# Attention probabilities turned by VectorE and DRAM transfers instead of TensorE, in a two-layer hybrid model on one Trainium2 core

## The chip, the core and the metric

The kernel runs on one core of one Trainium2 chip. The metric is the device time of one execution in microseconds (us), taken as the median of several runs. The profile is one execution taken by the hardware profiler; its span, from the first instruction to the last, is a little shorter than the device time of the same execution.

The engines are named as the profile names them: PE is TensorE (PEld its weight loads), DVE is VectorE, ACT is ScalarE, POOL is GpSimd, SP is SyncE. SP issues the weight loads as DMAs. DMAs issued from POOL go through a queue of their own ("q0 software_dynamic" in the profile), those of SP through "q1 hardware_dynamic"; all run on the core's 16 DMA engines.

## The reference

A model of two layers over 512 tokens of width 1024, all in float32. Layer one is attention over three groups of heads ("dilated" windows), layer two an mLSTM; each is followed by a SwiGLU network, and a norm ends it. Only the attention is touched here. Cut to what matters:

```python
proj = (xn @ w_in).reshape(B, S, 3, 3, 8, 128)           # group, q/k/v, head
for g, (window, dilation) in enumerate(((128, 1), (512, 4), (2048, 16))):
    q = rope(proj[:, :, g, 0]) * scale; k = rope(proj[:, :, g, 1]); v = proj[:, :, g, 2]
    s = where(valid, q @ k.T, -inf)      # banded, in blocks of 128
    p = exp(s - max(s)); den = sum(p)
    outs.append((p / den) @ v); lses.append(max(s) + log(den))
wts = softmax(stack(lses), axis=0)       # over the three groups
o = einsum('gbsh,gbshd->bshd', wts, stack(outs))
h = h + o.reshape(B, S, 1024) @ w_out
```

## The kernel before, in words

**Stages.** Activations are kept transposed (features on the 128 partitions, 512 tokens in the free dimension). Every projection is a product in three parts of rounded operands: a weight chunk of 512 KB (four row blocks of 128, 256 columns) is loaded by SP (line 200), split into a high part by ACT (line 208) and a low part by DVE (line 209), and multiplied by PE as high by high, high by low and low by high (lines 239 and 271). Three buffers of each kind (`W_BUFS`) let the load and the split run ahead of PE. A "tick" is one such chunk; `advance()` counts them, and `defer(n, fn)` runs `fn` once n more ticks have passed.

**Attention.** `attention_pair(pr)` (line 529) treats two heads at a time, four times. It projects q and k of the three groups (12 chunks), then v of the three groups (6 chunks). The work on the scores is deferred and falls among these chunks: `scores0` and `scores12` (products, masks, row maxima, exponentials), then `weigh` (exchange of maxima and sums between layouts, then one factor per row and block on DVE, lines 638 and 641), `turn` (values of group 0 turned by PE), `transposes(i)` for each of the pair's two heads and `values(i)`. The ticks are in `RUN_AT` (line 36), and in `LAST_AT` for the last pair. `run` and `fenced` hold PE's work of such a piece together at its place in the order.

**The turn of the probabilities.** A head has 15 blocks of 128 by 128 probabilities: 7 of group 0 (`p0`) and 4 each of groups 1 and 2 (`p12`). The values product contracts over keys, so each block is needed with the keys on the partitions. `transposes(i)` (line 652) turns 15 blocks on PE into four PSUM banks, and ACT copies each bank to SBUF (line 660) into one of four `pt` buffers. `values(i)` (line 663) multiplies: 7 products for group 0 (line 672), 8 for groups 1 and 2 (line 677), into the one PSUM bank of tag `t`; ACT copies the result to `oT` (line 679). As there are four `pt` buffers, the second head's blocks are turned after the first head's values product, in the same piece.

**The end of the attention.** For the last pair the pieces stand at the last v chunks and in the first chunk of the output projection. Lines 741 to 747 split six heads' outputs into high and low parts (lines 223, 224) before that projection, and the last two in a deferred piece. `out_project` (line 754) makes one column group of 256 after the other: two chunks, two accumulators.

**The start.** Line 108 keeps PE busy with 9 idle products while the first data come.

**Order.** Each engine works strictly in its own order; the build places instructions on each engine by their priority and an estimate of when they are ready. Tiles with one tag share `bufs` buffers in turn.

Of the kernel before, what the change touches and what calls it, by code (L numbers as in the profile page):

```python
# [11 lines left out]
F32 = mybir.dt.float32  # L12
# [58 lines left out]
def tile_hybrid_dilated_attn_mlstm(  # L71
# [33 lines left out]
    def idle(n):  # L105
        for i in range(n):
            nc.tensor.matmul(idle_ps, ones_r, idle_w, start=True, stop=True)
# [126 lines left out]
    def multiply(acc, whl, pairs, ch, m, nk):  # L234

        for k in range(min(4, nk - 4 * ch)):
            kk = 4 * ch + k
            for a, b in SPLITS:
                nc.tensor.matmul(  # L239
                    acc, whl[a][:, k, m * P:(m + 1) * P], pairs[b][kk],  # L240
                    start=(kk == 0 and (a, b) == SPLITS[0]),
                    stop=(kk == nk - 1 and (a, b) == SPLITS[-1]))
# [78 lines left out]

    with ExitStack() as actx:
        ap = pool(actx, "attn")

        R = 32
        mask_part = cst[:, K_MB:K_MB + 4]
        acst = ap.tile([P, K_END - K_MA], F32, name="acst")
        part = lambda at, w: acst[:, at - K_MA:at - K_MA + w]
        mask_band, mask_causal, mask_dil, perm = part(K_MA, 2 * P), part(K_M1, P), part(K_M2, P), part(K_G, P)
        cosn = ap.tile([R, SEQ], F32, name="cosn")  # L330
        sinn = ap.tile([R, SEQ], F32, name="sinn")
        sinr = ap.tile([R, SEQ], F32, name="sinr")

        posi = ap.tile([P, SEQ], I32, tag="rt", name="posi", bufs=2)
# [31 lines left out]
                nc.gpsimd.tensor_copy(cosn[:, c * P:(c + 1) * P], cs[s])  # L366

        def tok_tile(name):
            return ap.tile([P, 2, SEQ], F32, tag="qk", name=name, bufs=8)


        xtok = ap.tile([P, TB, D], F32, tag="heads", name="x_tok")
# [58 lines left out]

        def squares(hf):
            for tb in range(TB):
                sq = ap.tile([P, 512], F32, tag="v", name="x_sq", bufs=4)
# [94 lines left out]
        def attention_pair(pr):  # L529
# [6 lines left out]
            p0, p12, pts, vt = {}, {}, {}, []  # L536

            def score_bank(i, name):
                return ps.tile([P, 512], F32, tag="so"[i], name=name, bufs=2)
# [1 line left out]
            def scores0(q, k):  # L541

                for i in range(2):
                    p0[i] = ap.tile([P, 7, P], F32, tag="p0", name="%sp0_%d" % (nm, i), bufs=2)
                    for b2 in range(2):
                        sp = score_bank(i, "%ss0" % nm)
                        o, parts = 0, []
                        for b in (2 * b2, 2 * b2 + 1):
                            lo_ = max(b - 1, 0) * P
                            w = (b + 1) * P - lo_  # L550
                            nc.tensor.matmul(sp[:, o:o + w], q[:, i, b * P:(b + 1) * P],
                                             k[:, i, lo_:lo_ + w], start=True, stop=True)
                            parts.append((b, o, w))
                            o += w
                        for b, o, w in parts:
                            pb = max(2 * b - 1, 0)
                            nc.vector.tensor_tensor_reduce(
                                p0[i][:, pb:pb + w // P, :].rearrange("p a b -> p (a b)"),
                                sp[:, o:o + w], mask_band[:, 2 * P - w:], 1.0, -3e38,
                                op0=ALU.add, op1=ALU.max, accum_out=own[:, 0, 0, i, b:b + 1])  # L560
                for i in range(2):
                    exponentials(0, i)

            def scores12(qk1, qk2):

                for i in range(2):
                    p12[i] = ap.tile([P, 8, P], F32, tag="p12", name="%sp12_%d" % (nm, i), bufs=2)
# [49 lines left out]
            def weigh():  # L617

                exchange()
                cf = ap.tile([P, 16], F32, tag="cf", name=nm + "cf", bufs=2)  # L620
# [12 lines left out]
                cf4 = cf.rearrange("p (o i b) -> p o i b", o=2, i=2)  # L633
                for i in range(2):
                    for b in range(4):
                        pb = max(2 * b - 1, 0)
                        blk = p0[i][:, pb:2 * b + 1, :].rearrange("p a b -> p (a b)")
                        nc.vector.tensor_scalar(blk, blk, cf4[:, 0, i, b:b + 1], None, op0=ALU.mult)
                    for c in range(4):
                        blk = p12[i].rearrange("p (g c) k -> p c g k", g=2)[:, c]  # L640
                        nc.vector.tensor_scalar(blk, blk, cf4[:, 1, i, c:c + 1], None, op0=ALU.mult)

            def turn():
                for i in range(2):
# [17 lines left out]

            def values(i):
                pt = pts[i]
                hs = slice(i * P, (i + 1) * P)
                op = ps.tile([P, 512], F32, tag="t", name=nm + "o", bufs=1)
                first = True
                for b in range(4):
                    for kb in range(max(b - 1, 0), b + 1):
                        idx = 2 * b - (b - kb)  # L670
                        src = pt[idx // 4][:, (idx % 4) * P:(idx % 4 + 1) * P]
                        nc.tensor.matmul(by_block(op)[:, b], vt[0][:, kb, hs], src,
                                         start=first, stop=False, skip_group_check=True)
                        first = False
                for g in (1, 2):
                    for c in range(4):
                        nc.tensor.matmul(op[:, c * P:(c + 1) * P], vt[g][:, c, hs], pt[1 + g][:, c * P:(c + 1) * P],
                                         start=False, stop=(g == 2 and c == 3), skip_group_check=True)
                nc.scalar.activation(o_head(2 * pr + i), op, AF.Copy)

            qks = []
            for g in range(3):
# [30 lines left out]
                if g == 0:  # L713
                    defer(RUN_AT[0], lambda: run(lambda: scores0(*qks[0])))
            later_runs = (
                (lambda: scores12(*qks[1:]),), (weigh, turn),
                (lambda: transposes(0),), (lambda: values(0), lambda: transposes(1)), (lambda: values(1),))
            for at, fns in zip(RUN_AT[1:] if pr < HEADS // 2 - 1 else LAST_AT, later_runs):
                defer(at, lambda fns=fns: run(*fns))
            for g in range(3):  # L720
                v = ap.tile([P, TB, 256], F32, tag="v", name="%sv%d" % (nm, g), bufs=4)
                vt.append(v)

                def evac_v(m, acc, v=v):
# [10 lines left out]
                    project(pair, w_in, 2 * D + pr * 256, KC, evac_f, nm + "g0v")  # L735
                else:
                    project_tokens(pair, w_in, g * 3 * D + 2 * D + pr * 256, evac_v, "%sg%dv" % (nm, g))

        for pr in range(HEADS // 2):
            attention_pair(pr)  # L740
# [4 lines left out]
        def last_heads():  # L745
            for k in range(HEADS - 2, HEADS):
                split_act(pair[0][k], pair[1][k], o_head(k), None)

        def add_to_h(c):
            def evac(m, acc):  # L750
# [469 lines left out]
```

## Time and profile before

| | us |
|---|---|
| median of 3 runs | 1479.23 (1479.03 to 1479.31) |
| device time of the profiled execution | 1479.76 |
| its span | 1478.0 |
| PE busy | 1467.8 |
| DVE busy | 769.0 |
| ACT busy | 544.9 |
| POOL busy | 103.4 |

A row of the profile's groups reads: line, engine, operation, output<-inputs, shapes, count | busy time of the group, mean duration of one | idle time of the engine before them. PE's products are pipelined: each is listed with its full duration and they overlap, so what one costs PE is the distance from its start to the next start. A group's busy time is the union of its instructions. A row of the timeline has start, length, engine, line, operation; neighbours of one kind are merged with their count, and a bracket at the end tells the idle time before and what ended it. A row of the DMA view has the size of one transfer in KB and the median time from its issue to its landing. Of the span, the attention with its output projection takes the first 525 us.

### The profile page before, as it was taken

How to read it: one execution, taken by the hardware profiler on the slowest of the kernel's cores; microseconds unless marked ns; L12 is line 12 of the kernel's file. 1: busy time of each engine (PE TensorE's matmuls, PEld its weight loads, DVE VectorE, ACT ScalarE, POOL GpSimd, SP SyncE). 2: the span in 40 equal slices, each digit the busy share in tenths (PEclk: the TensorE clock that was granted, in tenths of full speed). 3: DMA queues.
4: the chain of work that ended last, by engine and by line, in shares of the span. 5: the costliest groups of instructions: out<-in, count | busy, mean ns of one | idle time of the engine just before them, and what ended most of it. 6: DMA issues, size and time to landing. Idle time of an engine off the chain costs nothing. (4 is left out here: it accounts for less than half of the span.)

```text
span 1478.0 us, 18932 instructions
## 1 busy us (share of the span) xinstructions
PE 1467.8 (99%) x7497; PEld 1253.0 (85%) x7497; DVE 769.0 (52%) x1515; ACT 544.9 (37%) x997; POOL 103.4 (7%) x95
## 2 busy tenths in 40 slices
PE   9999999999999999999999999999999999999998
PEld 7899889889889888888888889798888888888887
DVE  8744654654665463444343338987755443343233
ACT  5343225225216342333222223785542333233223
POOL 1000000000000001111110000000000111110001
PEclk9999999999999999999999999999999999999999
DMA  6222222232232233333323232232233233332231
GB/s 199 86 86 72 86 86 73 85 100 72 72 100 72 73 97 102 90 96 100 100 91 95 93 98 83 62 97 58 81 105 100 90 96 100 100 93 93 86 100 72
DMA packets 128466, 134.45 MB, mean 91 GB/s; under 512 B 5429, under 2 KB 121461, under 8 KB 128377
## 3 DMA queue, kind: packets, MB, share of 16 engines
q1 hardware_dynamic: 126384, 131.55, 28.7%
q8 instruction: 59, 0.97, 0.3%
q10 hardware_dynamic: 1656, 1.12, 0.2%
q0 software_dynamic: 336, 0.57, 0.1%
q14 instruction: 31, 0.25, 0.1%
HBM read 131.12 MB, written 2.10 MB: 90 GB/s over the span
## 5 line engine op out<-in xcount | busy, mean ns | idle before, releaser
L239 PE MATMUL f0j<-n_h,f0j_h 128*128 128x512 f32 x352 | 137.1, 389 | 0.0
L239 PE MATMUL f1j<-n_h,f1j_h 128*128 128x512 f32 x352 | 137.1, 389 | 0.0
L239 PE MATMUL f0j<-n_h,f0j_l 128*128 128x512 f32 x352 | 137.0, 389 | 0.0
L239 PE MATMUL f1j<-n_h,f1j_l 128*128 128x512 f32 x352 | 137.0, 389 | 0.0
L239 PE MATMUL f0j<-n_l,f0j_h 128*128 128x512 f32 x352 | 136.9, 389 | 0.0
L239 PE MATMUL f1j<-n_l,f1j_h 128*128 128x512 f32 x352 | 136.9, 389 | 0.0
L209 DVE TENSOR_TENSOR f1j_l<-f1j_w,f1j_h 128x1024 fp32r<-128x1024 f32 x44 | 54.9, 1247 | 54.5 <-ACT f1j_h L208 54.5
L209 DVE TENSOR_TENSOR f0j_l<-f0j_w,f0j_h 128x1024 fp32r<-128x1024 f32 x44 | 54.8, 1245 | 54.5 <-ACT f0j_h L208 54.5
L239 PEld LDWEIGHTS f0j<-n_h,f0j_l 128*128 128x128 f32 x352 | 66.1, 188 | 13.9
L239 PEld LDWEIGHTS f1j<-n_h,f1j_l 128*128 128x128 f32 x352 | 66.1, 188 | 13.8
L239 PEld LDWEIGHTS f1j<-n_h,f1j_h 128*128 128x128 f32 x352 | 66.1, 188 | 13.8
L239 PEld LDWEIGHTS f0j<-n_h,f0j_h 128*128 128x128 f32 x352 | 66.1, 188 | 13.8
L239 PEld LDWEIGHTS f1j<-n_l,f1j_h 128*128 128x128 f32 x352 | 66.1, 188 | 13.5
L239 PEld LDWEIGHTS f0j<-n_l,f0j_h 128*128 128x128 f32 x352 | 66.1, 188 | 13.5
L208 ACT ACTIVATE f1j_h<-f1j_w 128x1024 fp32r<-128x1024 f32 x44 | 46.5, 1057 | 73.3 <-PE f1j L239 72.2
L208 ACT ACTIVATE f0j_h<-f0j_w 128x1024 fp32r<-128x1024 f32 x44 | 46.5, 1057 | 73.3 <-PE f0j L239 72.2
L1152 PE MATMUL fin<-fw_h,f1ah 128*128 128x512 f32 (+1 forms) x198 | 72.8, 368 | 0.0
L1152 PE MATMUL fin<-fw_l,f1ah 128*128 128x512 f32 (+1 forms) x198 | 72.5, 366 | 0.0
L1152 PE MATMUL fin<-fw_h,f1al 128*128 128x512 f32 (+1 forms) x198 | 72.4, 366 | 0.0
L239 PE MATMUL fo<-f0ah,fo_k_h 128*128 128x512 f32 x176 | 68.5, 389 | 0.0
L239 PE MATMUL fo<-f0al,fo_k_h 128*128 128x512 f32 x176 | 68.5, 389 | 0.0
L239 PE MATMUL fo<-f0ah,fo_k_l 128*128 128x512 f32 x176 | 68.5, 389 | 0.0
(1167 smaller groups left out, 3579.8 us busy)
## 6 DMA issues: line engine op xcount, KB each, us to landing
f0j_w<-in_ffn_w_in_dram SPq DMA_DIRECT2D x44, 512.0 KB, 3.6
f1j_w<-in_ffn_w_in_dram SPq DMA_DIRECT2D x44, 512.0 KB, 3.5
fw_w<-in_ffn_w_out_dram SPq DMA_DIRECT2D x22, 512.0 KB, 3.8
fo_k_w<-in_ffn_w_out_dram SPq DMA_DIRECT2D x20, 512.0 KB, 3.4
awo_k_w<-in_attn_w_out_dram SPq DMA_DIRECT2D x8, 512.0 KB, 3.4
mv_k_w<-in_mlstm_w_in_dram SPq DMA_DIRECT2D x8, 512.0 KB, 3.6
mqk_k_w<-in_mlstm_w_in_dram SPq DMA_DIRECT2D x8, 512.0 KB, 3.7
mo_k_w<-in_mlstm_w_in_dram SPq DMA_DIRECT2D x8, 512.0 KB, 4.0
```

The source lines that it names most:

```text
L208: nc.scalar.activation(hi[:, :n], raw[:, :n], AF.Copy)
L209: nc.vector.tensor_tensor(lo[:, :n], raw[:, :n], hi[:, :n].bitcast(F32), op=ALU.subtract)
L239: nc.tensor.matmul(acc, whl[a][:, k, m * P:(m + 1) * P], pairs[b][kk], start=(kk == 0 and (a, b) == SPLITS[0]), stop=(kk == nk - 1 and (a, ...
L1152: nc.tensor.matmul(acc[i][:, cs], a[a_][kk][:, tb * P:(tb + 1) * P], whl[b_][:, k, cs], start=(kk == 0 and (a_, b_) == SPLITS[0]), stop=(k ...
```

## The change

- `transposes(i)` no longer uses PE and ACT. One DVE instruction turns all 15 blocks of a head, but only within squares of 32 by 32 (`nc.vector.transpose`), into a tile `pB`. Four DMAs, issued from POOL, write it to a DRAM tile `d`, one for each quarter of the partitions; a new function `bring(i)` reads it back with one DMA from POOL, arranged so that the squares stand in their places: 128 partitions, 1920 numbers each (983 KB).
- `values(i)` reads a block from this tile as four runs of 32 numbers, 480 numbers apart, instead of 128 neighbours, and writes into a bank of tag `o` (two buffers) instead of `t` (one).
- `weigh` is divided: `joint()` (the exchange and the factors), and `weigh(i)` for each head, so that the first head's blocks can leave before the second's are weighted. The issue order is joint, turn, weigh(0), transposes(0), weigh(1), transposes(1), bring(0), bring(1), all in one piece at tick 5; both heads' values follow at tick 10.
- For the last pair, the values products stand in the output projection. Its first two column groups are done together: chunk 0 of both, then blocks 4 and 5 of group 0, values of head 6, blocks 4 and 5 of group 1, values of head 7, then block 6 and block 7 of both. The two heads are split straight from PSUM.
- Buffers: `p0`, `p12` and `pB` share three buffers `p`; `pt` goes from four to two (shared with the rotary tables), `qk` from 8 to 6, `v` from 4 to 3.
- Ten idle products at the start instead of nine.

In the compiled order, DVE's turn of a pair's first head stands right behind the first factor of the second head; the turn of the second head stands behind the rest of the second head's factors and one low part of the next pair's weights (for the last pair: one low part of an output head).

```diff
-PT_BUFS = 4
-RUN_AT = (2, 3, 5, 6, 7, 8)
-LAST_AT = (2, 4, 5, 6, 7)
+RUN_AT = (2, 3, 5, 10)
+LAST_AT = (2, 4)
...
-    idle(9)
+    idle(10)
...
+        dp = pool(actx, "scratch", space=bass.MemoryType.DRAM)
...
+            p = [ap.tile([P, 15, P], F32, tag="p", name="%sp%d" % (nm, i), bufs=3) for i in range(2)]
+            p0, p12 = [t[:, :7] for t in p], [t[:, 7:] for t in p]
...
             def transposes(i):
-                pts[i] = []
-                for b, (src, n0, n1) in enumerate(((p0[i], 0, 4), (p0[i], 4, 7), (p12[i], 0, 4), (p12[i], 4, 8))):
-                    tp = score_bank(b // 2, nm + "pT")
-                    for j in range(n0, n1):
-                        transpose_into(tp, j - n0, src[:, j, :])
-                    t = ap.tile([P, 512], F32, tag="pt", name=nm + "pTs", bufs=PT_BUFS)
-                    w = (n1 - n0) * P
-                    nc.scalar.activation(t[:, :w], tp[:, :w], AF.Copy)
-                    pts[i].append(t)
+                t = ap.tile([P, 4, 15, R], F32, tag="p", name=nm + "pB", bufs=3)
+                nc.vector.transpose(t.rearrange("p b n i -> p n b i"), p[i])
+                d = pts[i] = dp.tile([4, R, 4, 15 * R], F32, tag="d", name=nm + "pD", bufs=2)
+                for a in range(4):
+                    nc.gpsimd.dma_start(d.rearrange("b j a x -> a j b x")[a],
+                                        t[R * a:R * (a + 1)].rearrange("p b n i -> p b (n i)"))
+
+            def bring(i):
+                pt = ap.tile([P, 4, 15, R], F32, tag="pt", name=nm + "pT", bufs=2)
+                nc.gpsimd.dma_start(pt.rearrange("p a n i -> p (a n i)"), pts[i].rearrange("b j a x -> (b j) (a x)"))
+                pts[i] = pt
...
-                op = ps.tile([P, 512], F32, tag="t", name=nm + "o", bufs=1)
+                op = ps.tile([P, 512], F32, tag="o", name=nm + "o", bufs=2)
...
-                        nc.tensor.matmul(by_block(op)[:, b], vt[0][:, kb, hs], src,
+                        nc.tensor.matmul(by_block(op)[:, b], vt[0][:, kb, hs], pt[:, :, 2 * b - (b - kb), :],
...
             later_runs = (
-                (lambda: scores12(*qks[1:]),), (weigh, turn),
-                (lambda: transposes(0),), (lambda: values(0), lambda: transposes(1)), (lambda: values(1),))
+                (lambda: scores12(*qks[1:]),),
+                (joint, turn, lambda: weigh(0), lambda: transposes(0), lambda: weigh(1), lambda: transposes(1),
+                 lambda: bring(0), lambda: bring(1)))
+            if pr < HEADS // 2 - 1:
+                later_runs += ((lambda: values(0), lambda: values(1)),)
...
-        defer(1, last_heads)
-        out_project(pair, attn_w_out[0], KC, "awo", end=1)
+        for c in range(2):
+            out_part(c, out_weights(c, 0), 0)
+        whl = [out_weights(c, 1) for c in range(2)]
+        for i in range(2):
+            out_part(i, whl[i], 1, (0, 1))
+            run(lambda: last_values(i, head_split))
+        for k in range(2, 4):
+            for c in range(2):
+                out_part(c, whl[c], 1, (k,), k == 3)
-    out_project(pair, attn_w_out[0], KC, "awo", first=1)
+    out_project(pair, attn_w_out[0], KC, "awo", first=2)
```

More of the change, by code (lines that the diff above doesn't have):

```diff
@@ L232, in x_tiles, with multiply @@
         return hi, lo
-    def multiply(acc, whl, pairs, ch, m, nk):
-        for k in range(min(4, nk - 4 * ch)):
+    def multiply(acc, whl, pairs, ch, m, nk, ks=None):
+        for k in ks or range(min(4, nk - 4 * ch)):
             kk = 4 * ch + k
@@ L329, in tile_hybrid_dilated_attn_mlstm @@
         mask_band, mask_causal, mask_dil, perm = part(K_MA, 2 * P), part(K_M1, P), part(K_M2, P), part(K_G, P)
-        cosn = ap.tile([R, SEQ], F32, name="cosn")
-        sinn = ap.tile([R, SEQ], F32, name="sinn")
+        cosn, sinn = (ap.tile([R, SEQ], F32, tag="pt", name=nm, bufs=2) for nm in ("cosn", "sinn"))
         sinr = ap.tile([R, SEQ], F32, name="sinr")
@@ L368, in tok_tile @@
         def tok_tile(name):
-            return ap.tile([P, 2, SEQ], F32, tag="qk", name=name, bufs=8)
+            return ap.tile([P, 2, SEQ], F32, tag="qk", name=name, bufs=6)
         xtok = ap.tile([P, TB, D], F32, tag="heads", name="x_tok")
@@ L535, in attention_pair @@
             oth = ap.tile([P, 2, 2, 2, 4], F32, tag="oth", name=nm + "oth", bufs=2)
-            p0, p12, pts, vt = {}, {}, {}, []
+            p = [ap.tile([P, 15, P], F32, tag="p", name="%sp%d" % (nm, i), bufs=3) for i in range(2)]
+            p0, p12 = [t[:, :7] for t in p], [t[:, 7:] for t in p]
+            pts, vt, weight = {}, [], []
             def score_bank(i, name):
@@ L632, in weigh @@
                 nc.vector.tensor_tensor(cf, cf, ee[:, 0], op=ALU.mult)
[L633 to L641, printed above, removed]
+                weight.append(cf.rearrange("p (o i b) -> p o i b", o=2, i=2))
+            def weigh(i):
+                cf4 = weight[0]
+                for b in range(4):
+                    pb = max(2 * b - 1, 0)
+                    blk = p0[i][:, pb:2 * b + 1, :].rearrange("p a b -> p (a b)")
+                    nc.vector.tensor_scalar(blk, blk, cf4[:, 0, i, b:b + 1], None, op0=ALU.mult)
+                for c in range(4):
+                    blk = p12[i].rearrange("p (g c) k -> p c g k", g=2)[:, c]
+                    nc.vector.tensor_scalar(blk, blk, cf4[:, 1, i, c:c + 1], None, op0=ALU.mult)
             def turn():
@@ L676, in values @@
                     for c in range(4):
-                        nc.tensor.matmul(op[:, c * P:(c + 1) * P], vt[g][:, c, hs], pt[1 + g][:, c * P:(c + 1) * P],
+                        nc.tensor.matmul(op[:, c * P:(c + 1) * P].rearrange("p (a i) -> p a i", a=4),
+                                         vt[g][:, c, hs], pt[:, :, 3 + 4 * g + c, :],
                                          start=False, stop=(g == 2 and c == 3), skip_group_check=True)
-                nc.scalar.activation(o_head(2 * pr + i), op, AF.Copy)
+                if out is None:
+                    nc.scalar.activation(o_head(2 * pr + i), op, AF.Copy)
+                else:
+                    out(2 * pr + i, op)
             qks = []
@@ L737, in attention_pair @@
                     project_tokens(pair, w_in, g * 3 * D + 2 * D + pr * 256, evac_v, "%sg%dv" % (nm, g))
+            return values
         for pr in range(HEADS // 2):
-            attention_pair(pr)
+            last_values = attention_pair(pr)
         pair = x_tiles("ao")
@@ L743, in tile_hybrid_dilated_attn_mlstm @@
             split_act(pair[0][k], pair[1][k], o_head(k), None)
-        def last_heads():
-            for k in range(HEADS - 2, HEADS):
-                split_act(pair[0][k], pair[1][k], o_head(k), None)
         def add_to_h(c):
@@ L756, in out_project, with out_part, out_weights @@
                 project(pairs, w2d, c * 256, nk, add_to_h(c), "%s%d" % (name, c))
-        defer(1, last_heads)
-        out_project(pair, attn_w_out[0], KC, "awo", end=1)
         assert not later
-    out_project(pair, attn_w_out[0], KC, "awo", first=1)
+        acc = [[acc_tile("awo0_%d" % m) for m in range(2)],
+               [ps.tile([P, 512], F32, tag="s", name="awo1_%d" % m, bufs=2) for m in range(2)]]
+        def out_part(c, whl, ch, ks=None, last=False):
+            for m in range(2):
+                with fenced():
+                    multiply(acc[c][m], whl, pair, ch, m, KC, ks)
+                if last:
+                    add_to_h(c)(m, acc[c][m])
+        def out_weights(c, ch):
+            return split_chunk(weight_chunk(attn_w_out[0], ch, c * 256, 4, "awo%d_k%d" % (c, ch)))
+        head_split = lambda k, op: split_act(pair[0][k], pair[1][k], op, None)
+        for c in range(2):
[8 more added lines that the diff above has]
+    out_project(pair, attn_w_out[0], KC, "awo", first=2)
     def norm(key, k0, name):
```

12 lines of the change are left out of this document (4 added, 8 removed).

## The prediction

> **What bounds the kernel now.** I read the page first (busy time, granted clock, chain), then PE's waits, then PE's timeline around one pair of heads.
>
> ```profile
> PE 1467.8 (99%) x7497; PEld 1253.0 (85%) x7497; DVE 769.0 (52%) x1515; ACT 544.9 (37%) x997; POOL 103.4 (7%) x95
> ...
> PEclk9999999999999999999999999999999999999999
> ...
> PE 35%; DVE 3%; issue 0%; ACT 0%; DVEq 0%; ACTq 0%
> ```
>
> ```profile
> PE idle L107 <- DVE idle_w L102: 1.5, 1, 1.5
> PE m0s L1035 <- DVE ks L1007: 0.7, 1, 0.7
> PE m0s L1035 <- DVE m0e L1037: 0.7, 1, 0.7
> PE a0g0q L426 <- ACT first_h L416: 0.4, 1, 0.4
> ```
>
> PE is busy 99% of the span at full granted clock, and it waits 3.3 us in all, none of it in the attention after the start. So every microsecond of PE's issue that goes is a microsecond of the end, and every wait that comes is one too. The other engines matter only where PE comes to wait for them. PE's timeline around the first pair's turn shows what an edit is worth there:
>
> ```profile
> 120.07 1.80 PE L282 MATMUL a0pT<-cst,a0p 128*128 128x128 f32 x15
> 121.63 0.48 PE L239 MATMUL a1g0q<-xa_h,a1g0q_k_h 128*128 128x512 f32 x1
> 121.94 0.40 PE L239 MATMUL a1g0q<-xa_l,a1g0q_k_h 128*128 128x512 f32 x1
> 122.17 0.39 PE L239 MATMUL a1g0q<-xa_h,a1g0q_k_l 128*128 128x512 f32 x1
> ...
> 127.17 1.73 PE L672 MATMUL a0o<-a0pTs,a0v 128*128 128x128 f32 x14
> ...
> 130.52 1.80 PE L282 MATMUL a0pT<-cst,a0p 128*128 128x128 f32 x15
> 132.08 0.48 PE L239 MATMUL a1g0q<-xa_h,a1g0q_k_h 128*128 128x512 f32 x1
> ...
> 137.61 1.73 PE L672 MATMUL a0o<-a0pTs,a0v 128*128 128x128 f32 x14
> ```
>
> Fifteen turns last from 120.07 to 121.63: **1.56 us of issue**, not 15 x 0.272. Back to the projection, the first step is 0.31 us instead of the usual 0.23: each interruption costs 0.08 more. A chunk between two interruptions lasts 5.53 us (132.08 to 137.61), so 5.45 without. One values product (14 + 16 records) with what follows it lasts 3.35 us (127.17 to 130.52).
>
> **The change, part by part.**
>
> *Turns leave PE.* 8 heads x 1.56 = **-12.5 us**. The other pairs cost the same, as the groups of the first and the last pair show:
>
> ```profile
> L282 PE MATMUL a3pT<-cst,a3p 128*128 128x128 f32 x30 | 3.6, 272 | 0.0
> L282 PE MATMUL a0pT<-cst,a0p 128*128 128x128 f32 x30 | 3.6, 272 | 0.0
> L677 PE MATMUL a0o<-a0pTs,a0v 128*128 128x128 f32 x32 | 3.9, 275 | 0.0
> L672 PE MATMUL a0o<-a0pTs,a0v 128*128 128x128 f32 x28 | 3.5, 275 | 0.0
> ```
>
> *Fewer interruptions.* Three per pair before (turn; values and turn; values), one after; in the last pair two instead of three. 7 x 0.08 = **-0.6 us**.
>
> *Values read runs of 32 numbers.* No product of before reads its moving operand in runs, so I bound it. Line 672 writes its result in runs of 32 and line 677 in one piece, and both last 275 ns: runs on the writing side cost nothing. I take 0. If the runs halved the rate, the 7.4 us of busy time per pair (3.9 + 3.5) would double: up to +29.6 us. A gain is excluded, since the counts and sizes stay.
>
> *ACT's copies of the turned blocks* go. ACT was no bound, so 0. The o banks have two buffers, and scores of the next pair come two ticks after the values: 0.
>
> *DVE's turn* is a new instruction of 1920 numbers per partition. Its nearest rows are shuffles, which rearrange partitions within 32 in one pass:
>
> ```profile
> L512 DVE STREAM_SHUFFLE rot<-a0g1k 32x512 f32<-32x512 f32 x2 | 1.4, 725 | 0.0
> ...
> 3.93 0.30 DVE L347 STREAM_SHUFFLE angles<-angles 128x128 f32<-128x128 f32 x1
> ```
>
> From 128 to 512 numbers 0.425 us are added, 1.107 ns each; 1920 numbers give 0.725 + 1408 x 0.0011 = **2.28 us**. Bounds: 2.0 (7.5 times the 0.265 us step of line 641's factors of 256 numbers, below) and 4.6 (each square filled, then drained, twice the passes). I take 2.28. The Trainium skill, page "VectorE: DVE Perf Modes", section "The three transpose paths", gives 311 ns for a 128x128 block in 2-byte numbers and advises TensorE for such blocks. As an estimate from that page, 15 x 311 ns = 4.7 us. With that the sum below would be about 5 us smaller; no run here shows either.
>
> *What the turns delay on DVE.* Here are the last pair's factors (lines 638, 641) and what stands behind them, and PE's end of the v projection:
>
> ```profile
> 461.33 1.07 DVE L638 TENSOR_SCALAR a3p<-a3p,a3cf 128x128 f32<-128x128 f32 x4
> 462.32 1.13 DVE L641 TENSOR_SCALAR a3p<-a3p,a3cf 128x256 f32<-128x256 f32 x4
> 463.38 1.07 DVE L638 TENSOR_SCALAR a3p<-a3p,a3cf 128x128 f32<-128x128 f32 x4
> 464.36 1.13 DVE L641 TENSOR_SCALAR a3p<-a3p,a3cf 128x256 f32<-128x256 f32 x4
> 465.41 2.49 DVE L224 TENSOR_TENSOR ao_l<-oT,ao_h 128x512 fp32r<-128x512 f32 x4
> 467.82 1.22 DVE L209 TENSOR_TENSOR awo_k_l<-awo_k_w,awo_k_h 128x1024 fp32r<-128x1024 f32 x1
> ...
> 472.61 1.72 PE L672 MATMUL a3o<-a3pTs,a3v 128*128 128x128 f32 x14
> ```
>
> In the new order DVE does: factors of head 6, one factor of head 7 (463.63), turn (465.91), other factors (467.69), one low part of an output head at 0.62 us (468.31), turn (470.59), five more low parts (473.69), then the first low part of the output weights: ready at **474.9**, against about 469.0 before. PE ends the v projection at 472.61 less the first turn, 471.05, and no values or turns stand between it and the output projection any more. It can do 8 products without that low part (8 x 0.23 = 1.8, to 472.9) and then waits **+2.0 us**. With a turn of 2.0 us it waits 1.4, with 4.6 us 6.6. In the other pairs the low part behind the turn is wanted two chunks later (11 us), so the turns' 4.6 us hide under PE's chunks.
>
> *The round trip* (five POOL transfers per head). The nearest rows:
>
> ```profile
> awo_k_w<-in_attn_w_out_dram SPq DMA_DIRECT2D x8, 512.0 KB, 3.4
> ...
> out_dram<-ht SPq DMA_DIRECT2D x4, 256.0 KB, 2.1
> ...
> gbc<-in_final_norm_dram POOLq DMA_DIRECT2D x1, 512.0 KB, 5.3
> acst<-in_shape_constants_dram SPq DMA_DIRECT2D x1, 320.0 KB, 7.7
> ...
> rows<-in_mlstm_conv_w_dram POOLq DMA_DIRECT2D x1, 16.0 KB, 5.8
> ```
>
> ```profile
> q1 hardware_dynamic: 126384, 131.55, 28.7%
> ```
>
> ```profile
> 1068.46 0.61 POOL L1117 DMA_DIRECT2D gbc<-in_final_norm_dram  x1 [79.41 <-PE mwo L239]
> ```
>
> POOL takes 0.61 us to issue, and lands 1.9 us later than SP for the same size (5.3 against 3.4). A quarter (246 KB) out: 2.1 + 1.9 = 4.0 us (bounds 2.1 and 5.8). The 983 KB back: q1 moved 131.55 MB in 28.7% of 1478 us, 310 GB/s, so 459 KB more than gbc add 1.5: 6.8 us (bounds 5.3; 9.9 in proportion to gbc; 23 in proportion to acst, which landed in the rush of the start). On POOL's queue the first head's return stands behind the second head's four departures. First pair, with DVE's steps as above from its start there:
>
> ```profile
> 117.25 1.07 DVE L638 TENSOR_SCALAR a0p<-a0p,a0cf 128x128 f32<-128x128 f32 x4
> ...
> 123.94 1.23 DVE L209 TENSOR_TENSOR a1g0k_k_l<-a1g0k_k_w,a1g0k_k_h 128x1024 fp32r<-128x1024 f32 x1 [2.52 <-ACT a1g0k_k_h L208]
> ```
>
> The first turn ends at 121.8, the second, behind the low part of line 209, at 127.1; its departures are issued by 129.5, so head 0 is back at 136.3; head 1's last quarter lands at 132.9 and head 1 is back at 139.7. PE wants them four chunks after 120.07: 120.07 + 5.53 + 3 x 5.45 = 141.95, and 145.3. **Margin 5.6 us: no wait.** In the last pair head 6 is back at 473.0 + 6.8 = 479.8 and wanted at 474.9 + 9.1 + 2.7 = 486.7, margin 6.9. The weights have been loaded by then one to two chunks ahead, so sharing the 16 engines costs 0.
>
> *Last pair's values between halves of chunks.* Head 7's low part is needed 2.7 us after its values end; ACT and DVE need about 0.6 + 0.7: 0. *Tenth idle product*:
>
> ```profile
> 1.52 4.21 PE L107 MATMUL idle<-idle_w,ones_r 128*128 128x512 f32 x9 [1.52 <-DVE idle_w L102]
> ```
>
> Nine end at 5.73; a tenth adds at most 4.21/9 = 0.47, part of it while PE waits for data anyway. I take +0.1.
>
> **Sum**: -12.5 - 0.6 + 2.0 + 0.1 = **-11.0 us**. Against the profiled execution, 1479.76, that is 1468.8; the median of before stands 0.5 lower, so I predict **1468.2 us**. Anything under 0.2% (3.0 us) can't be told from no change.
>
> **The rivals.**
>
> *A. The forecast*, 1466.1 (no wait at the output projection) to 1470.5: **0.62**.
>
> *B. DVE's turn at half rate*, 4.6 us. For it: every square must be full before it can be read crosswise. Against: the shuffles keep one pass. The wait at the output projection becomes 6.6, the round trip is still just in time (head 0 back at 141.0): 1472.8. **0.13**.
>
> *C. The round trip is late by a little.* If DVE's work keeps POOL from issuing until the second turn has ended (127.1), and the transfers take their upper POOL bounds (5.8 and 9.9), head 0 is back at 144.6, 2.7 us late in three pairs, and 1.4 late in the last: 9.5 us of waits, 1477.7; with milder bounds less. For it: POOL lands slower than SP in every row. Against: both bounds must hold. The Trainium skill, page "SBUF — State Buffer", section "Who interferes with whom", states such a lock between VectorE's faster modes and GpSimd, and that descriptors of GpSimd's DMAs wait for it; no row of before can show it. **0.12**.
>
> *D. The round trip is far late; slower than before.* Place: the values products, in PE's order behind the return. It decides when a return takes 8.7 us longer than I took, over 15.5 us (three times 3.1 beyond the margin of 5.6, once 1.8 beyond 6.9, is 11). In proportion to acst, 23 us: head 0 back at 152.6, waits of 10.6 three times and 9.4 once, 41 us, 1509. For it: bursts of 983 KB beside weight loads. Against: acst's row is from a stretch where everything loaded at once. **0.08**.
>
> *E. Reading runs costs PE.* At half rate +29.6 - 11.0: 1498. **0.05**, partly between.
>
> That PE would keep the turns is excluded: its compiled order has none of these blocks left.
>
> **How the numbers follow.** A is likeliest: 1468.2. A, B and the milder half of C hold 0.81 between 1466 and 1475; that is the range. Faster: A, B, two thirds of C, 0.83; within 0.2%: the rest of C and a little of E, 0.06; slower: D and most of E, 0.11.
>
> **What would show it.** Right: no PE record of the turn's names; values products of 275 ns; one wait of PE at the output projection of about 2 us, put down to DVE's low part; DVE's turn at 2.3 us; no wait of PE at the values. Wrong: PE waits at the values put down to DMA (C, D), values steps over 0.12 us (E), or a turn near 4.6 us (B).

## The result and the profile after

The changed kernel takes **1468.05 us** (median of 4 runs, 1467.44 to 1468.29), the kernel before beside it 1479.27 (1479.03 to 1479.64): a ratio of 0.9923, 95% interval 0.9906 to 0.994. The profiled execution took 1467.84 us with a span of 1466.1, 11.9 less than before.

The page of the changed kernel, its busy times, granted clock and chain:

```profile
PE 1454.4 (99%) x7378; PEld 1239.4 (85%) x7378; DVE 784.7 (54%) x1523; ACT 528.5 (36%) x963; POOL 125.3 (9%) x135
...
PEclk9999999999999999999999999999999999999999
...
PE 36%; DVE 3%; issue 0%; ACT 0%; DVEq 0%; ACTq 0%
```

PE is still the bound. It has lost 13.4 us of busy time, DVE has gained 15.7 and POOL 21.9 (mostly its DMA issues). Of PE's waits in the same execution (total us, times, longest) these are the longest after the start:

```profile
PE awo L238 <- DVE awo_k_l L208: 1.4, 1, 1.4
PE m0s L1062 <- DVE ks L1034: 0.7, 1, 0.7
```

The first is new. It is the one that the prediction put at the output projection. No row names a DMA: the values never wait for the round trip. PE's timeline of the first pair's values shows it:

```profile
141.44 0.40 PE L238 MATMUL a1g0k<-xa_h,a1g0k_k_l 128*128 128x512 f32 x1
141.67 1.73 PE L675 MATMUL a0o<-a0pT,a0v 128*128 128x128 f32 x14
...
145.02 1.73 PE L675 MATMUL a0o<-a0pT,a0v 128*128 128x128 f32 x14
...
148.29 0.48 PE L238 MATMUL a1g1q<-xa_h,a1g1q_k_h 128*128 128x512 f32 x1
```

Values start 0.23 us after the last projection product, one head's products take 3.35 us as before (145.02 less 141.67), and no turn stands between. The groups of the new and the changed instructions:

```profile
L657 DVE STREAM_TRANSPOSE a1pB<-a1p 128x1920 f32<-128x1920 f32 x2 | 4.3, 2168 | 0.0
L680 PE MATMUL a0o<-a0pT,a0v 128*128 128x128 f32 x32 | 3.9, 275 | 0.0
...
L675 PE MATMUL a0o<-a0pT,a0v 128*128 128x128 f32 x28 | 3.5, 275 | 0.0
```

DVE's turn takes 2.17 us. A product that reads runs of 32 numbers takes 275 ns, as one that reads 128 neighbours did. POOL's timeline of the first pair:

```profile
121.77 2.22 POOL L660 DMA_DIRECT2D a0pD<-a0pB  x4 [107.27 <-DVE a0pB L657]
126.80 2.18 POOL L660 DMA_DIRECT2D a0pD<-a0pB  x4 [2.81 <-DVE a0pB L657]
129.13 0.56 POOL L665 DMA_DIRECT2D a0pT<-a0pD  x1
135.80 0.55 POOL L665 DMA_DIRECT2D a0pT<-a0pD  x1 [6.11 <-DMA a0pD<-a0pB]
```

Then the DMA view of this kernel, cut to the issue of each of the two returns (129 to 130 us, and 135.7 to 136); the last column is the time from issue to landing:

```profile
a0pT<-a0pD POOLq DMA_DIRECT2D x1, 960.0 KB, 9.7
```

```profile
a0pT<-a0pD POOLq DMA_DIRECT2D x1, 960.0 KB, 6.9
```

Head 0 is back at 129.13 + 9.7 = 138.8 and wanted at 141.67: a margin of 2.8 us. Head 1 is back at 135.80 + 6.9 = 142.7 and wanted at 145.02: 2.3. The prediction had 5.6 for both. So its sign was right here with half the room. The stretches around it (length, then busy time of PE, PEld, DVE, ACT and POOL with counts, granted clock, share of the 16 DMA engines, GB/s):

```profile
121.00:124.00 3.00, 3.00 (x15) 2.45 (x15) 3.00 (x9) 0.87 (x1) 2.22 (x4) 1.00 0.40 78
124.00:127.00 3.00, 3.00 (x15) 2.49 (x14) 3.00 (x3) 1.06 (x1) 0.20 (x1) 1.00 0.90 233
...
133.00:136.00 3.00, 3.00 (x14) 2.46 (x14) 2.85 (x4) 0.00 (x0) 0.20 (x1) 1.00 1.04 411
...
139.00:142.00 3.00, 3.00 (x16) 2.53 (x15) 1.46 (x4) 0.36 (x1) 0.00 (x0) 1.00 0.96 340
```

From 124 to 142 us the DMA engines are full (0.98 busy over the whole stretch); in the kernel before they were 0.21 busy over the same stretch. The weights of the next pair are loaded amid this. The DMA view of the changed kernel from 100 to 150 us:

```profile
a1g1q_k_w<-in_attn_w_in_dram SPq DMA_DIRECT2D x2, 512.0 KB, 6.1
a1g1k_k_w<-in_attn_w_in_dram SPq DMA_DIRECT2D x2, 512.0 KB, 7.6
```

These loads took 3.5 and 3.6 us in the kernel before. They are requested early enough that PE doesn't notice.

### The profile page after: what moved, and what is told of

It is laid out like the page before. It is cut to its first block, busy times and chain, and to the rows that moved or that the text cites. A ratio compares the mean times of both kernels' runs of the same rounds, so it can differ in the third digit from the quotient of the medians.

```text
span 1466.1 us, 18728 instructions
## 1 busy us (share of the span) xinstructions
PE 1454.4 (99%) x7378; PEld 1239.4 (85%) x7378; DVE 784.7 (54%) x1523; ACT 528.5 (36%) x963; POOL 125.3 (9%) x135
## 3 DMA queue, kind: packets, MB, share of 16 engines
q1 hardware_dynamic: 126384, 131.55, 28.8%
```

## The experiments

The theory to be tested: the 11.4 us are PE's issue of the turns and their interruptions (13.1), less a wait of 1.4 to 1.6 at the output projection, with the tenth idle product at about 0.2 in favour. The rivals: the gain comes from the new order; the margin of the round trip is as wide as predicted; the wait at the output projection is DVE's amount of work and not its order.

### The tenth idle product alone

```diff
-    idle(9)
+    idle(10)
```

> The kernel before with ten idle products instead of nine, and nothing else. Read from the two traces: in the changed kernel PE's first projection product starts at 8.92 us instead of 9.12, so the tenth idle product should gain 0.2 us by itself: about 1479.1, not to be told from no change by time, but PE's first product of a0g0q in the trace should start at about 8.9. The recorded prediction gave it +0.1 (at most +0.47): then that product starts at 9.2 to 9.6.

1479.61 us (1478.89 to 1479.97), the kernel before 1479.33 (1478.87 to 1479.88); ratio 1.0, interval 0.9991 to 1.0009. PE's timeline at the start:

```profile
6.09 1.09 PE L282 MATMUL xT<-cst,x_tok 128*128 128x128 f32 x8
...
8.63 0.50 PE L426 MATMUL a0g0q<-xa_h,first_h 128*128 128x512 f32 x1 [0.51 <-ACT first_h L416]
```

The eight turns of x last 1.09 us here, 1.97 before, and the projection starts at 8.63, before at 9.12. So in this one execution the product that was to cost 0.1 seems to gain 0.5. But the start scatters: in the twelve profiles with ten idle products the projection starts anywhere from 8.09 to 9.27 us, and the one profile with nine, at 9.12, lies within that. The medians lean the other way, 0.3 slower with the tenth, and can't show so little. Sign and size of this small term stay open.

### The turns back on PE, all else as in the changed kernel

```diff
-    (joint, turn, lambda: weigh(0), lambda: transposes(0), lambda: weigh(1), lambda: transposes(1),
-     lambda: bring(0), lambda: bring(1)))
+    (joint, turn, lambda: weigh(0), lambda: weigh(1)),
+    (lambda: transposes(0),), (lambda: transposes(1),))
...
-RUN_AT = (2, 3, 5, 10)
-LAST_AT = (2, 4)
+RUN_AT = (2, 3, 5, 6, 7, 10)
+LAST_AT = (2, 4, 5, 6)
```

Here `transposes` turns on PE and lets ACT copy, as in the kernel before, and the values read 128 neighbours.

> The changed kernel with its order of work, its interleaved output projection and its tenth idle product, but with the turns back on PE and ACT, one and two ticks after the factors; DVE's turns and the round trip are gone. Theory (the gain is PE's issue of the turns): +12.5 for eight turns, +0.5 for six more interruptions, -1.4 because DVE no longer keeps the first low part of the output weights back: 1468.05 + 11.6 = 1479.6, between 1478.8 and 1480.5, with no wait of PE over 0.3 us at the output projection. Rival (the gain comes from the new order or from the interleaved output projection, and PE's turns were hidden in gaps): 1470 or less.

1479.01 us (1478.69 to 1479.65), ratio 0.9998 (0.9989 to 1.0007) to the kernel before. PE's timeline in the first pair:

```profile
119.61 1.80 PE L281 MATMUL a0pT<-cst,a0p 128*128 128x128 f32 x15
121.16 0.48 PE L238 MATMUL a1g0q<-xa_h,a1g0q_k_h 128*128 128x512 f32 x1
```

The turn issues in 1.55 us again and nothing waits at the output projection. The rival "the order brings the gain" falls: order, interleaving, buffers and idle product together are worth nothing that can be told. On the same chip the version of the next section, which has no wait at the output projection either but DVE's turns, takes 1466.39 us: 12.6 us lie between the two.

### The first low part of the output weights ahead of five others

```diff
-        for k in range(HEADS - 2):
-            split_act(pair[0][k], pair[1][k], o_head(k), None)
...
+        head_split(0, o_head(0))
+        first = out_weights(0, 0)
+        for k in range(1, HEADS - 2):
+            head_split(k, o_head(k))
         for c in range(2):
-            out_part(c, out_weights(c, 0), 0)
+            out_part(c, first if c == 0 else out_weights(c, 0), 0)
```

> The changed kernel with the first low part of the output weights ahead of the low parts of heads 1 to 5 on DVE. Theory (the 1.43 us wait at the output projection is those five low parts of 0.61 us standing ahead of it behind the second turn): awo_k_l starts at about 460.1 instead of 463.0, PE waits 0 to 0.5 us there, and the time is 1466.6 to 1467.1 (1468.05 less 0.9 to 1.4). Rival (the wait is DVE's total amount of work there, so that another low part comes late in its place): PE waits 1.2 us or more for ao_l parts, and the time stays at 1468.

1466.39 us (1465.98 to 1466.46), ratio 0.991 (0.9897 to 0.9924) to the kernel before. First the timelines of PE and of DVE at the output projection in the changed kernel, then the same of this one:

```profile
462.48 0.39 PE L238 MATMUL awo<-ao_l,awo_k_h 128*128 128x512 f32 x1
464.30 0.50 PE L238 MATMUL awo<-ao_h,awo_k_l 128*128 128x512 f32 x1 [1.43 <-DVE awo_k_l L208]
```

```profile
457.97 2.17 DVE L657 STREAM_TRANSPOSE a3pB<-a3p 128x1920 f32<-128x1920 f32 x1
460.06 3.05 DVE L223 TENSOR_TENSOR ao_l<-oT,ao_h 128x512 fp32r<-128x512 f32 x5
463.04 3.48 DVE L208 TENSOR_TENSOR awo_k_l<-awo_k_w,awo_k_h 128x1024 fp32r<-128x1024 f32 x3
```

```profile
461.14 0.40 PE L238 MATMUL awo<-ao_l,awo_k_h 128*128 128x512 f32 x1
461.38 0.45 PE L238 MATMUL awo<-ao_h,awo_k_l 128*128 128x512 f32 x1
```

```profile
460.10 1.18 DVE L208 TENSOR_TENSOR awo_k_l<-awo_k_w,awo_k_h 128x1024 fp32r<-128x1024 f32 x1
461.20 3.08 DVE L223 TENSOR_TENSOR ao_l<-oT,ao_h 128x512 fp32r<-128x512 f32 x5
```

The low part is ready 2.9 us sooner, the five others follow just as fast as PE needs them, and the wait is gone. The gain, 1.6, is more than the 1.43 that the list of waits names, because a listed wait begins where the modelled end of the product before it lies. From start to start PE lost 464.30 - 462.48 - 0.23 = 1.59 us. That is the number to count with.

### The changed kernel and this version side by side

> The changed kernel once more, on the same chip as the next one: 1468.0, with 1467.4 to 1468.6 for single runs.

> The version with the first low part ahead, beside the changed kernel on the same chip: 1.6 us less (the step from 462.48 to 464.30 instead of 0.23 us), 1466.4, its runs all below those of the changed kernel.

On one chip: the changed kernel 1467.84 us (1467.24 to 1468.06, ratio to the kernel before 0.9923, 0.9911 to 0.9936), the other 1466.27 (1466.07 to 1466.51, ratio 0.9914, 0.99 to 0.9927). Their runs don't overlap. This version beats both kernels.

### The values one chunk earlier

```diff
-RUN_AT = (2, 3, 5, 10)
+RUN_AT = (2, 3, 5, 9)
```

> The changed kernel with the values of the first three pairs one chunk (5.45 us) earlier. Recorded prediction: a margin of 5.6 us, so no wait, 1468. Theory from the trace of the changed kernel: head 0 is back at 129.13 + 9.7 = 138.8 and head 1 at 135.80 + 6.9 = 142.7; with the values wanted at 136.2, PE waits 2.6 us for head 0 and then 0.5 for head 1, 3.1 us in each of three pairs, put down to DMA: 1468.05 + 9.3 = 1477.4, between 1475 and 1480.

1478.3 us (1477.71 to 1481.64): 10.3 above the changed kernel, almost all of the gain. PE's timeline at the values of pairs 0 and 1:

```profile
136.12 0.39 PE L238 MATMUL a1g0k<-xa_h,a1g0k_k_l 128*128 128x512 f32 x1
138.23 1.83 PE L675 MATMUL a0o<-a0pT,a0v 128*128 128x128 f32 x14 [1.72 <-DMA a0pT<-a0pD]
...
142.97 1.83 PE L675 MATMUL a0o<-a0pT,a0v 128*128 128x128 f32 x14 [1.12 <-DMA a0pT<-a0pD]
...
255.42 2.80 PE L675 MATMUL a1o<-a1pT,a1v 128*128 128x128 f32 x14 [1.87 <-DMA a1pT<-a1pD]
258.01 2.65 PE L680 MATMUL a1o<-a1pT,a1v 128*128 128x128 f32 x16
260.50 1.73 PE L675 MATMUL a1o<-a1pT,a1v 128*128 128x128 f32 x14
```

In pair 0 PE loses 1.88 for head 0 and 142.97 - 138.23 - 3.35 = 1.39 for head 1, 3.3 together, close to the expected 3.1. The predicted margin of 5.6, which would have covered this, falls. In pair 1 there is one wait, but the values behind it are slow: 260.50 - 255.42 = 5.08 us instead of 3.35. The windows of that stretch say why (the mean granted clock is the third number from the end):

```profile
255.40:258.00 2.60, 2.58 (x14) 2.58 (x15) 0.28 (x1) 0.00 (x0) 0.00 (x0) 0.63 0.94 337
258.00:260.50 2.50, 2.50 (x19) 2.50 (x18) 0.00 (x0) 0.00 (x0) 0.00 (x0) 0.71 0.70 246
260.50:263.00 2.50, 2.50 (x25) 2.50 (x24) 0.00 (x0) 0.60 (x1) 0.00 (x0) 1.00 0.05 13
```

Over the 5 us after the wait the mean granted clock is 0.63 and 0.71. In finer windows there is nothing between: it is 1.00 until 256.1, 0.50 from there to 259.5, and 1.00 again. In pairs 0 and 2 it stayed at 1.00 after waits of 1.72 and 2.10 us.

### DVE's turn done twice

```diff
                 nc.vector.transpose(t.rearrange("p b n i -> p n b i"), p[i])
+                nc.vector.transpose(t.rearrange("p b n i -> p n b i"), p[i])
```

> The changed kernel with each of DVE's turns done twice over, so that a turn costs 4.3 us, as the recorded rival B had it. Recorded: +4.3 of wait at the output projection and nothing at the values, about 1472.4. Theory from the trace of the changed kernel, where head 0 came back 2.9 us and head 1 2.3 us before it was wanted: head 0's return moves 4.3 us, to 143.1, and is 1.5 late, head 1's is then about 0.5 late, in three pairs, +6 more: 1478.3, between 1475 and 1482, with waits of PE put down to DMA at the values of pairs 0 to 2.

1481.16 us (1480.25 to 1483.19), ratio 1.0014 (1.0005 to 1.0024): slower than before the change. Some of PE's waits that differ from the changed kernel:

```profile
PE awo L238 <- DVE awo_k_l L208: 5.6, 1, 5.6
PE a1o L676 <- DMA a1pT<-a1pD: 1.9, 2, 1.2
...
PE a0o L676 <- DMA a0pT<-a0pD: 1.1, 2, 0.6
```

The wait at the output projection grew by 4.2, as both accounts had it. The six waits at the values, 4.6 together with pair 2's 1.6, are those of the narrow margin and were not in the recorded price of rival B. These waits are 8.8 of the 13.1 us. The time still lies 3 us above the expected 1478.3, within the range named. The granted clock was 0.50 from 472.8 to 479.6 us; PE got on at 474.3, and its products then start 0.43 us apart instead of 0.23, so that about 2.7 us more are lost there (an estimate: half of the 5.4 us).

### The second head's return first

```diff
-                 lambda: bring(0), lambda: bring(1)))
+                 lambda: bring(1), lambda: bring(0)))
```

> The changed kernel with head 1's return issued ahead of head 0's, so that no return runs beside head 1's departures. If the 16 DMA engines are full from the first departure to the last landing (they are busy 0.96 to 1.04 of the time from 127 to 142 us), the order changes little in when the last byte lands: head 1's departures land near 133.3 instead of 135.7, both returns are back at 141.5 to 143, head 0 up to 1 us late, 1468 to 1471. If instead each transfer has a long fixed time on POOL's queue, both are back by 140.5 and PE never waits: 1468.

1481.65 us, with runs from 1476.86 to 1488.19; ratio 1.0021 (1.0006 to 1.0036). POOL's timeline in the first pair of the profiled run (one of the two longest), and PE's longest wait:

```profile
135.82 1.17 POOL L665 DMA_DIRECT2D a0pT<-a0pD  x2 [6.57 <-DMA a0pD<-a0pB]
```

```profile
PE a0o L675 <- DMA a0pT<-a0pD: 4.1, 1, 4.1
```

POOL gets on at 135.82, in the changed kernel at 135.80. From the first issue that is 8.8 us without head 0's return beside head 1's departures and 9.0 with it, so my expectation of 133.3 fell, and with it the idea that this return holds them up. What the return did beside them was almost free. Put behind them, head 0 is back only near 146.2, where PE's wait ends, and not by 143, and PE waits 4.1, 4.1, 3.0 and 2.8 us in the four pairs. In the profiled execution, 20 us above the changed kernel, the granted clock was also at 0.50 from 146.9 to 150.3, after the first pair's wait. The wide spread of the runs was not followed further.

### One head's round trip only

```diff
-                for a in range(4):
+                for a in range(4 if i == 0 else 0):
...
+                if i == 1:
+                    pts[1] = pts[0]
+                    return
```

> The changed kernel without the round trip of each pair's second head: its departures and its return are left out, and its values read the first head's probabilities. If head 0's return took 9.7 us because it shares the DMA engines with head 1's departures, it takes 5.3 to 7 us here (recorded: 6.8); if 983 KB on POOL's queue need that long by themselves, 9 us or more. The time stays at 1468 either way, or 0.5 below.

1468.7 us in one run. The DMA view at the return's issue:

```profile
a0pT<-a0pD POOLq DMA_DIRECT2D x1, 960.0 KB, 6.7
```

Alone beside the weight loads, 983 KB come back in 6.7 us, against 9.7 beside head 1's departures; in the other pairs it is 7.0, 7.2 and 5.5 against 9.4, 9.7 and 8.0. So the size taken for a return, 6.8, was right for a lone one, and the sharing between the two heads is what was left out: 2.4 to 3.0 us. The return doesn't simply stand behind the departures on POOL's queue: in the changed kernel's first pair that queue moved 0.89 + 0.19 MB before the return's issue at 129.13 and 1.63 MB from there to 135.80, when the last departure had landed. Both heads' departures are 1.97 MB, so about 0.7 MB of the return's 0.98 had moved beside them.

### The last values ahead of the output projection

```diff
+        for i in range(2):
+            run(lambda: last_values(i, head_split))
         for c in range(2):
             out_part(c, out_weights(c, 0), 0)
         whl = [out_weights(c, 1) for c in range(2)]
         for i in range(2):
             out_part(i, whl[i], 1, (0, 1))
-            run(lambda: last_values(i, head_split))
```

> The changed kernel with the last pair's values ahead of the whole output projection, and not amid it. Theory (the first chunks of the output projection hide the last round trip): PE is done with the v projection at 460.9, head 6 is back at 462.64 + 8.0 = 470.6 and head 7 at 467.09 + 8.1 = 475.2, so PE waits 9.7 us, does 3.35 of values, waits 1.2; the 1.6 lost for the first low part goes, and 0.1 to 0.2 of interruptions: 1468.05 + 9.1 = 1477.1, up to 1480 if the clock drops after so long a wait. Rival (the interleaving hides nothing, the round trip is done by then): 1466.5 to 1468.

1478.93 us (1477.84 to 1480.44), ratio 0.9999 (0.999 to 1.0009): the whole gain is gone. PE's timeline and windows there:

```profile
470.02 3.32 PE L675 MATMUL a3o<-a3pT,a3v 128*128 128x128 f32 x14 [9.73 <-DMA a3pT<-a3pD]
473.13 3.04 PE L680 MATMUL a3o<-a3pT,a3v 128*128 128x128 f32 x16
476.01 1.73 PE L675 MATMUL a3o<-a3pT,a3v 128*128 128x128 f32 x14
```

```profile
470.30:473.00 2.70, 2.70 (x14) 2.70 (x14) 0.00 (x0) 0.00 (x0) 0.00 (x0) 0.50 1.08 415
473.00:475.50 2.50, 2.50 (x14) 2.50 (x14) 0.00 (x0) 0.00 (x0) 0.00 (x0) 0.52 0.82 281
```

A wait of 9.7 us as expected, and then head 6's values at half the clock, 5.99 us instead of 3.35. Those 2.64 cover head 7's expected wait of 1.2, which leaves 1.4 above 1477.1: 1478.5, against a median of 1478.93. The profiled execution is the fastest of the ten, 1477.84. So the interleaving is worth nothing by itself (the turns back on PE showed that) and 10.9 us once the last pair needs a round trip.

### Short runs on the return instead of the departure

On top of the version with the first low part ahead:

```diff
-                for a in range(4):
-                    nc.gpsimd.dma_start(d.rearrange("b j a x -> a j b x")[a],
-                                        t[R * a:R * (a + 1)].rearrange("p b n i -> p b (n i)"))
+                nc.gpsimd.dma_start(d.rearrange("a j b x -> (a j) (b x)"), t.rearrange("p b n i -> p (b n i)"))
...
-                nc.gpsimd.dma_start(pt.rearrange("p a n i -> p (a n i)"), pts[i].rearrange("b j a x -> (b j) (a x)"))
+                for b in range(4):
+                    nc.gpsimd.dma_start(pt[R * b:R * (b + 1)].rearrange("p a n i -> p a (n i)"),
+                                        pts[i].rearrange("a j b x -> b j a x")[b])
```

> On top of the version with the first low part ahead (1466.4): the DRAM scratch is laid out so that a head leaves in one transfer with 7,680 bytes in a row per partition and comes back in four transfers that read 1,920 bytes at a time; before it left in four transfers with 1,920 bytes in a row and came back in one. Same bytes, five transfers per head either way. If the short runs are what made the departures land late (last one 6.6 us after its issue, at 230 to 290 GB/s, where the returns moved 340 to 410), the departure lands within 5 us of its issue and the returns become the slow half, and both heads are back within a microsecond of 138.8 and 142.7. If writing to DRAM is slow whatever the runs, the departure still needs 6 us or more. The time stays at 1466.4 in both, since there is a margin of 2 us, unless head 1 comes back after 145: then up to 3 us a pair more.

1469.29 us (1468.2 to 1469.85), 3.0 above the version that it builds on, with small waits at the values (0.7 us the longest). The profiled execution, 1468.2, is the fastest of the four, so it shows only a part of the 3.0. The windows in which the first pair's returns run:

```profile
136.00:139.00 3.00, 3.00 (x15) 2.46 (x14) 1.26 (x2) 1.06 (x1) 0.00 (x0) 1.00 1.10 269
139.00:142.00 3.00, 3.00 (x17) 2.57 (x16) 1.61 (x4) 0.54 (x1) 0.00 (x0) 1.00 1.03 209
```

The engines are as full as in the changed kernel and move 209 to 269 GB/s where it moved 340 and 357 in the same windows: returns in four transfers that read runs of 1,920 bytes are slower. That the length of the run is the reason isn't shown. The weight loads move 131.55 MB in 126,384 packets, about 1,040 bytes each, and took 28.7% of the kernel before, which is 310 GB/s; here the order of the addresses and the number of transfers changed as well. Head 0's departure as one transfer lands 4.1 us after its issue and head 1's 6.1, so only the first was within the 5 us expected of long runs. In the changed kernel head 0's four quarters took 2.9 to 5.0 each and head 1's 4.4 to 6.8, and each head's four 2.2 to issue. How much of a late departure is the short run, how much the four issues and how much the traffic beside it stays open.

## Why the prediction was right, step by step

- *Turns leave PE, fewer interruptions* (-12.5 and -0.6 predicted). Right. From the first projection product to the end of the span the kernel before takes 1478.0 - 9.12 = 1468.9 us, the version without the new wait 1464.5 - 8.77 = 1455.7 and the version with the turns back on PE 1477.2 - 8.49 = 1468.7. That leaves 13.2 and 13.0 for the two, where 13.1 was forecast. The medians of the last two, which hold the start with its scatter, differ by 12.6.
- *The wait at the output projection* (+2.0). Right in place and cause, a little too long: 1.59 from start to start. The low part came 3.35 us after the end of the v projection (463.04 + 1.18 = 464.22, less 460.87) instead of 3.85. Two turns of 2.17 instead of 2.28 are 0.22 of that half microsecond.
- *DVE's turn* (2.28, from the shuffles' slope). 2.17; rival B with 4.6 is out. So is the 4.7 us that was worked out as an estimate from the Trainium skill's page "VectorE: DVE Perf Modes", section "The three transpose paths": one large instruction is not fifteen small ones.
- *Strided reads* (0, up to +29.6). 0: 275 ns for either form; rival E is out.
- *The tenth idle product* (+0.1). Open. The first projection product starts at 8.92 instead of 9.12 in these two profiles, but at 8.09 to 9.27 in all those with ten products, and the medians of the experiment lean to a cost of 0.3.
- *The round trip* (no wait, margin 5.6). No wait, but the margin was 2.8 and 2.3. The term that was mis-sized is the landing: 4.0 for a quarter, measured 2.9 for the first of the first pair, 4.7 in the middle and 6.8 for the last, and 6.8 for a return, measured 9.7 for head 0 beside head 1's departures. "Sharing the 16 engines costs 0" held for PE's time alone.
- *Rival C's lock.* The windows of the changed kernel show DVE busy for all of 121 to 124 us, and POOL issuing four departures there in 2.22, 0.55 each. A lock of the kind that the Trainium skill's page "SBUF — State Buffer", section "Who interferes with whom", describes doesn't show in these rows. The first quarter, issued while DVE was busy, landed in 2.9 us, sooner than the 4.0 reckoned; the later ones were late while the DMA engines were 0.90 to 1.04 busy. That the full engines are the whole cause of it is argued and not shown.
- *Rivals B and D were priced too low.* With a turn of 4.3 us the kernel takes 1481.2, where B had 1472.8 for 4.6. Both rested on the margin of 5.6, and neither price had the half clock after a wait. And the point from which the round trip eats the gain is not a return 8.7 us longer but about 6, as an estimate: values 5.45 us earlier took 10.3 us of the gain.

Against the profiled execution the forecast was 1468.8, and it took 1467.84. Of these 0.9 us, 0.4 are the wait, reckoned too long, and 0.3 the start, in which these two executions differ by 0.2 the other way; the last 0.2 isn't assigned. In the medians the forecast came closer, 1468.2 and 1468.05, and that is partly luck: the gain is 11.9 us between the two profiled executions and 11.2 between the medians, because the profiled execution of the kernel before lies 0.5 above its median and that of the changed kernel 0.2 below its own. The wait was reckoned 0.3 to 0.4 too long by either count. In the medians something of about 0.2, the start or scatter, made up for half of it, and no run settles which. The cover over the round trip, on which no term of the sum depended, was half as thick as reckoned.

## What to carry to other kernels

Where one engine sets the time, work moved off it pays back its issue time (here 13.0 to 13.2 us, where 13.1 were reckoned), as long as what replaces it comes back before the bound engine asks; price the replacement by its transfers sharing the DMA engines with each other, not by a lone one. Look for the first instruction behind the moved work that the bound engine waits for, and put it ahead: here a different order of six low parts was worth another 1.6 us. Count a wait from start to start, and add what the clock does after it.

## What the runs showed of the hardware

- A short wait can cost more than its length. After some waits PE's granted clock was at 0.50 for a stretch, and in fine windows it is 1.00 or 0.50 with nothing between. The stretches lasted 3.4 us (256.1 to 259.5, values one chunk earlier, after a wait of 1.87 us), 3.4 (146.9 to 150.3, second head's return first, 4.12 us), 6.8 (472.8 to 479.6, turn done twice, 5.55 us) and 10.2 (465.2 to 475.4, last values ahead, 9.73 us): once, once, twice and three times 3.41. They don't begin with the wait. The first began 0.6 us after PE had got on, the last 4.9 us after PE had stopped, and PE lost 1.7 and 2.6 us of work by these two. Waits of 1.72 and 2.10 us left the clock at 1.00. The Trainium skill's page "TensorE: Matmul & The Clock Gate", section "Part 1: The HAM clock gate", has the clock halve after an idle window of about 3.4 us that runs freely. The half rate, the multiples of 3.4 us and the hit or miss agree with that; that a wait of 1.87 us can be enough doesn't follow from it, and the measurement stands. A reading that no run tests: if the windows of 3.41 us go on without a break, the 1.87 us lie within the one that ends at 256.1, and the 2.10 us of pair 2 (371.0 to 373.1) are split by an edge near 372.
- DVE turns 128 by 1920 four-byte numbers in squares of 32 in 2.17 us, 1.13 ns for each number of a partition.
- Full DMA engines are no rate: at 0.9 to 1.1 busy they moved from 209 to 415 GB/s here, least beside returns in four transfers with runs of 1,920 bytes.
